# A two-layer RWKV-7/mLSTM trunk on one core: the planner may go straight on to a small product that is due within one K tile, the program begins and ends differently, and two lags change

## The chip, the cores and the metric

The kernel runs on one core of one Trainium2 chip. The metric is the device time of a whole execution in microseconds (us). Three runs of the kernel before gave 2409.18, 2411.95 and 3999.0 us, median 2411.95.

## The reference

A trunk of two layers works on 512 frames of 1024 features, all in fp32. Each layer is a half-weighted SwiGLU block, a mixer block in which two token mixers (RWKV-7 with 8 heads of 64, mLSTM with 4 heads of 128) read one joint projection, and a second half-weighted SwiGLU block; a last RMSNorm follows.

```
for l in range(DEPTH):
    h = h + HALF * _swiglu(_rmsnorm(h, ffn1_norm[l]), ffn1_w_in[l], ffn1_w_out[l])
    xn = _rmsnorm(h, mix_norm[l])
    z = xn @ w_in[l]
    ...
    u = jax.nn.sigmoid(g_a) * (y_a @ br_a[l]) + jax.nn.sigmoid(g_b) * (y_b @ br_b[l])
    h = h + u @ w_out[l]
    h = h + HALF * _swiglu(_rmsnorm(h, ffn2_norm[l]), ffn2_w_in[l], ffn2_w_out[l])
return _rmsnorm(h, final_norm)
```

## The kernel before, in words

Activations lie transposed: features on the 128 partitions, the 512 frames along the free axis. A projection makes one block of 128 output features. Its weight block comes by DMA as `wraw`; ScalarE (ACT) rounds it to `whi`, VectorE (DVE) takes the rest `wlo` (`cut`, L425 and L426). For each of the 8 blocks of 128 input features (a K tile) TensorE (PE) then does three products, hi·hi, hi·lo and lo·hi (`product`, L461 to L463), into one PSUM bank. Two banks (pool `mm`) take projections, six (pool `mx`) everything small.

The program has five kinds of stages: `opening` (L437), where the first two weight blocks and the input arrive in pieces; the rest of the first SwiGLU (`ffn`); `mixers`; a second `ffn`; and after two layers the end in `run` (L1262 and on), a norm and eight multiplications, each followed by its DMA out.

In `mixers` a planner (`Weave`) writes TensorE's order out by hand. The small products (transposes, products of 64, 32 or 16 rows, sums over partitions) are threads that yield what they wait for: a time on the planner's own clock `t` ("at"), a flag, a lock or a projection. The planner resumes the first thread that is ready and, where none is, writes one K tile of a projection and adds `STEP` = 0.69 us to `t`. It charges 0.1 us for each turn from K tiles to small products and 0.1 us back. The "at" times come from lags written into the code: `wv.mark(latency, busy)` books DVE's time and returns the start plus the latency; ACT's queue is not booked. The other engines' orders follow from the order in which the code issues their instructions and from the scheduler.

The threads that the prediction speaks of: `mlstm_gates` (its lag of 16.0 stands ahead of the transposes of `rstd` and `ee`, helper line L684); `rwkv_chunks` (lag 3.2 between transposes and `rwkv_values`, L1163); `rwkv_gated` (L1231 and on: sums over heads by `sums`, L482 and L483, a subtraction L1238, a square L1239, a second `sums`, then `rsqrt`, which is Ln L517 and Exp L518, each behind a load of ACT's function table); `mlstm_head` (scores L798, their Relu and Exp L795 and L796); and `rwkv_out` (L1194, L1206 and the chain of states L1212, with copies L1199 that give its `mx` banks back). `table` (L511) asks for an Ln on a constant, to have the Ln table loaded early.

Of the kernel before, what the change touches and what calls it, by code (L numbers as in the profile page):

```python
# [13 lines left out]
AF = mybir.ActivationFunctionType  # L14
ALU = mybir.AluOpType
# [3 lines left out]
P = 128  # L19
# [4 lines left out]
KD = D // P  # L24
# [206 lines left out]
class Weave:  # L231
# [49 lines left out]
    def run(self):  # L281
        trunk = self.trunk
        job = None
        self.threads.sort(key=lambda th: th[0])
        while job or any(not th[3] for th in self.threads):
            th = next((th for th in self.threads if self.ready(th[2])), None)
            if th is not None:
                if th[2][0] == "lock":
                    self.held.add(th[2][1])
                self.resume(th)  # L290
                continue
            if job is None:
                th = next((th for th in self.threads if th[2][0] == "proj"), None)
                if th is not None:
                    job = [th, trunk.weights(th[2][1]), trunk.mm(), 0]
                    th[2] = ("job", None)
                    self.mark(0.0, 1.4)
            if job is not None:
                th, w, ps, k = job
                trunk.product(ps, w, k, trunk.xh[:, k, :], trunk.xl[:, k, :], k == 0, k == KD - 1)  # L300
                self.t += self.STEP + (0.1 if self.small else 0.0)
                self.small = False
                job[3] += 1
                if job[3] == KD:
                    job = None
                    self.resume(th, ps)
                continue
            times = [th[2][1] for th in self.threads if th[2][0] == "at"]
            times += [self.flags[th[2][1]] for th in self.threads if th[2][0] == "flag" and th[2][1] in self.flags]
            self.t = min(times)  # L310
# [19 lines left out]
class Trunk:  # L330
    def __init__(self, ctx, tc, a, out):
        self.tc, self.nc, self.a, self.out = tc, tc.nc, a, out
        pool = lambda n, b, **k: ctx.enter_context(tc.tile_pool(name=n, bufs=b, **k))
        self.pw = pool("weights", 3)
        self.pt = pool("tmp", 2)
        self.pmm = pool("mm", 2, space=PSUM)
        self.pmx = pool("mx", 6, space=PSUM)
        self.pd = pool("dram", 1, space=DRAM)
        self.keep = Scope(tc)
        nc = self.nc  # L340
        k = self.keep.tile
        self.xh = k((P, KD, T), F32R, "xh")
        self.xl = k((P, KD, T), F32R, "xl")
        self.rstd = k((P, T), F32, "rstd")
        self.acc = k((P, T), F32, "acc")
        self.cst = k((P, 4, P), F32, "cst")
        self.sel = k((P, 7, P), F32R, "sel")
        self.big = k((P, 512), F32, "big")
        self.fin = k((P, KD), F32, "fin")
        self.tid = k((P, 8, 16), F32, "tid")  # L350
        self.vec = [k((P, NCOL), F32, f"vec{l}") for l in range(L)]
        self.half = [k((P, NCOL), F32, f"half{l}") for l in range(L)]
        self.k256 = [k((P, 4), F32, f"k256_{l}") for l in range(L)]
        self.eps = k((P, 4), F32, "eps")
        self.onemu = [k((P, 15), F32, f"onemu{l}") for l in range(L)]

        k((P, 96), F32, "pad")
        self.sq, self.sl = (k((P, 512), F32R, n) for n in ("sq", "sl"))
        self.ld = [k((P, 512), F32, f"ld{i}") for i in range(2)]
        self.residual()  # L360
        for i, e in enumerate((RMS_EPS, GN_EPS, LN_EPS)):
            nc.gpsimd.memset(self.eps[:, i : i + 1], e)
        nc.scalar.copy(out=self.eps[:, 3:4], in_=self.eps[:, 0:1])
        nc.sync.dma_start(out=self.vec[0], in_=a["vec"][0])
        self.ident = self.cst[:, 0, :]
        dram = lambda n, k, s: [self.pd.tile(s, F32, name=f"{n}{i}", tag=f"{n}{i}") for i in range(k)]
        self.vfirst = dram("vfirst", 4, [P, T])
        self.bonus = dram("bonus", 4, [P, T])
        self.yd = dram("yd", 8, [P, T])
        self.hd = dram("hd", KD, [P, T])  # L370
        self.mxd = dram("mxd", 4, [64, 16, 16])
        self.gd = dram("gd", 16, [P, T])
        self.zd = dram("zd", 4, [P, 8, 16])
# [63 lines left out]
    def opening(self):  # L437

        nc, a = self.nc, self.a
        raw = [self.pw.tile([P, KD * P], F32, name="wraw", tag="wraw", bufs=2) for _ in range(2)]  # L440
        w = [self.parts() for _ in range(2)]
        ps = [self.mm() for _ in range(2)]
        for k in range(0, KD, 2):
            for i in (k, k + 1):
                (nc.gpsimd if i % 2 else nc.sync).dma_start(out=self.h[:, i, :], in_=a["xt"][:, i, :])
                self.feed(i, self.col(0, "g1", i))
                if i == k:
                    for j in range(2):
                        s = slice(k * P, (k + 2) * P)
                        nc.sync.dma_start(out=raw[j][:, s], in_=a["f1i"][0, 0, j, :, s])  # L450
                        self.cut(raw[j], w[j], k, k + 2)
            for i in (k, k + 1):
                for j in range(2):
                    self.product(ps[j], w[j], i, self.xh[:, i, :], self.xl[:, i, :], i == 0, i == KD - 1)
        return ps

    def product(self, ps, w, k, xh, xl, first, last):
# [52 lines left out]

    def table(self):  # L511

        self.nc.scalar.activation(out=self.eps[:, 3:4], in_=self.eps[:, 0:1], func=AF.Ln)

    def rsqrt(self, out, in_, eps, scale=1.0):
        nc = self.nc
# [11 lines left out]
    def ffn(self, l, m, done, first=None):  # L528
        nc = self.nc
        win, wout = self.a[f"f{m}i"], self.a[f"f{m}o"]  # L530
        sc = Scope(self.tc)
        hh = [sc.tile((P, T), F32R, f"hh{j}") for j in range(KF)]
        hl = [sc.tile((P, T), F32R, f"hl{j}") for j in range(KF)]
        for j in range(KF):
            if j == 0 and first is not None:
                pg, pu = first()
                self.norm()
            else:

                pg = self.project(win[l, j, 0], ps=self.mx() if j < 2 else None)  # L540
                if j == 0:
                    self.norm()
                pu = self.project(win[l, j, 1])
            if j == 2 and first is not None:
                self.constants()
            g = self.tmp("t0")
            nc.vector.tensor_tensor(out=g, in0=pg, in1=self.rstd, op=ALU.mult)  # L547
            s = self.tmp("t1", 1)
            nc.scalar.activation(out=s, in_=g, func=AF.Silu)  # L549
            p = self.tmp("t2", 1)  # L550
            nc.vector.tensor_tensor(out=p, in0=pu, in1=s, op=ALU.mult)  # L551
            self.split(hh[j], hl[j], p)
        for i in range(KD):
            ps = self.mm()
            for k0 in range(0, KF, KD):
                nk = min(KD, KF - k0)
                w = self.weights(wout[l, i, :, k0 * P : (k0 + nk) * P], nk)
                for k in range(nk):
                    j = k0 + k
                    self.product(ps, w, k, hh[j], hl[j], j == 0, j == KF - 1)  # L560
            t = self.tmp("t0")
            nc.vector.scalar_tensor_tensor(out=t, in0=ps, scalar=0.5, in1=self.rstd, op0=ALU.mult, op1=ALU.mult)
            nc.vector.tensor_tensor(out=self.h[:, i, :], in0=self.h[:, i, :], in1=t, op=ALU.add)  # L563
            done(i)
        sc.close()
# [136 lines left out]
    def mlstm_gates(self):  # L702

        nc, l, zm, wv = self.nc, self.l, self.zm, self.wv
# [18 lines left out]
        self.split(self.m_rc[I], self.m_rc[F], rc[I])  # L723
        nc.vector.tensor_tensor(out=rt[I], in0=rt[I], in1=rc[I], op=ALU.subtract)
        nc.scalar.activation(out=slab[F], in_=rt[I], func=AF.Exp)
        yield "at", wv.mark(16.0, 8.0)

        ps = self.mx()
        self.transposes(ps, [self.rstd[:, P * j : P * j + P] for j in range(4)])
        nc.vector.tensor_copy(out=self.m_rcol, in_=ps.rearrange("p (j c) -> p j c", j=4)[:, :, 0:1])  # L730
        ps = self.mx()
# [291 lines left out]
    def rwkv_chunks(self, p):  # L1023

        nc, l, k, a, kk, bk, wv = self.nc, self.l, self.r_k, self.r_a, self.r_kk, self.r_bk, self.wv
# [28 lines left out]
        at = wv.t + 3.0  # L1054
        for q in range(2):
# [14 lines left out]
            for hh in range(2):  # L1070
# [1 line left out]
                C = slice(8 * hh + 4 * q, 8 * hh + 4 * q + 4)  # L1072
                nc.scalar.copy(out=s3[0:64, C, wc : wc + CH], in_=ps4[0:64, :, wc : wc + CH])
                nc.scalar.copy(out=s3[64:128, C, yc : yc + CH], in_=ps4[64:128, :, yc : yc + CH])
            at = wv.t + 3.2
        yield "at", at
        self.rwkv_values(p)

# [183 lines left out]
    def run(self):  # L1262
# [39 lines left out]
        self.norm(self.last)  # L1302
        for i in range(KD):
            h = self.h[:, i, :]
            eng = nc.gpsimd if i in (2, 5) else nc.vector
            eng.tensor_tensor(out=h, in0=h, in1=self.rstd, op=ALU.mult)
            nc.sync.dma_start(out=self.out[i * P : i * P + P, :], in_=h)
        self.hs.close()
        self.keep.close()

# [10 lines left out]
```

## Time and profile before

| | us |
|---|---|
| median of three runs | 2411.95 |
| the profiled execution | 2413.39 |
| its span, first to last instruction | 2411.7 |
| PE busy | 2379.0 (99% of the span) |
| DVE busy | 1301.7 (54%) |
| ACT busy | 1062.1 (44%) |
| POOL busy | 109.4 (5%) |
| first product starts at | 8.21 |
| first of the last two matmuls starts at | 2397.57 |

The span is 1.7 us shorter than the profiled execution's time; the rest lies outside the first and last instruction. Matmuls are pipelined and their ends are modelled, so the distance between two starts tells what a matmul takes, and its duration does not. The first layer's mixers lie roughly between 380 and 750 us and the second's between 1570 and 1960 us.

### The profile page before, as it was taken

How to read it: one execution, taken by the hardware profiler on the slowest of the kernel's cores; microseconds unless marked ns; L12 is line 12 of the kernel's file. 1: busy time of each engine (PE TensorE's matmuls, PEld its weight loads, DVE VectorE, ACT ScalarE, POOL GpSimd, SP SyncE). 2: the span in 40 equal slices, each digit the busy share in tenths (PEclk: the TensorE clock that was granted, in tenths of full speed). 3: DMA queues.
4: the chain of work that ended last, by engine and by line, in shares of the span. 5: the costliest groups of instructions: out<-in, count | busy, mean ns of one | idle time of the engine just before them, and what ended most of it. 6: DMA issues, size and time to landing. Idle time of an engine off the chain costs nothing.

```text
span 2411.7 us, 33612 instructions
## 1 busy us (share of the span) xinstructions
PE 2379.0 (99%) x13044; PEld 1954.2 (81%) x13044; DVE 1301.7 (54%) x2340; ACT 1062.1 (44%) x1808; POOL 109.4 (5%) x155
## 2 busy tenths in 40 slices
PE   8999999999999999999999999999999999999997
PEld 7888888787788888888888888878877888888886
DVE  5444446876866644444444444478678665444433
ACT  5333336566565443333343333375565645333322
POOL 1000000000000100000000000000000001000012
PEclk9999999999999999999999999999999999999999
DMA  4223333323436322233323333433133353332332
GB/s 159 96 97 96 106 117 117 99 80 91 129 94 185 118 96 96 96 95 97 102 94 99 99 95 111 132 94 106 60 117 119 100 156 128 99 100 98 92 97 83
DMA packets 116799, 256.13 MB, mean 106 GB/s; under 512 B 40064, under 2 KB 43264, under 8 KB 116640
## 3 DMA queue, kind: packets, MB, share of 16 engines
q1 hardware_dynamic: 115696, 251.30, 33.5%
q8 instruction: 103, 1.69, 0.3%
q10 hardware_dynamic: 624, 1.64, 0.2%
q0 software_dynamic: 320, 1.05, 0.1%
q14 instruction: 56, 0.46, 0.1%
HBM read 230.88 MB, written 23.07 MB: 105 GB/s over the span
## 4 chain that ended last, share of the span: by engine, by line
PE 88%; DVE 6%; ACT 3%; issue 2%; DMA 1%; POOL 0%; DVEq 0%; SPq 0%; ACTq 0%; POOLq 0%
PE mm L461 27%; PE mm L463 26%; PE mm L462 26%; PE mx L1194 1%; DVE wlo L426 1%; PE mx L813 1%; PE mx L684 1%; PE mx L798 1%; PE mx L463 1%; PE mx L462 1%; PE mx L461 1%; DVE tz L1102 0%; DVE pr L1100 0%; PE mx L1182 0%; DVE qk L758 0%
## 5 line engine op out<-in xcount | busy, mean ns | idle before, releaser
L425 ACT CAST whi<-wraw 128x512 fp32r<-128x512 f32 (+1 forms) x800 | 487.2, 610 | 1030.1 <-PE mm L462 920.3
L426 DVE TENSOR_TENSOR wlo<-wraw,whi 128x512 fp32r<-128x512 f32 (+1 forms) x800 | 556.7, 697 | 593.3 <-ACT whi L425 590.2
L461 PE MATMUL mm<-xh,whi 128*128 128x512 f32 x2104 | 837.5, 398 | 8.2 <-ACT whi L425 8.2
L463 PE MATMUL mm<-xh,wlo 128*128 128x512 f32 x2104 | 822.7, 391 | 2.1 <-DVE wlo L426 2.1
L462 PE MATMUL mm<-xl,whi 128*128 128x512 f32 x2104 | 821.8, 391 | 0.0
L461 PEld LDWEIGHTS mm<-xh,whi 128*128 128x128 f32 x2104 | 396.6, 189 | 96.1 <-ACT whi L425 8.2
L463 PEld LDWEIGHTS mm<-xh,wlo 128*128 128x128 f32 x2104 | 396.3, 188 | 87.3 <-DVE wlo L426 2.9
L462 PEld LDWEIGHTS mm<-xl,whi 128*128 128x128 f32 x2104 | 396.8, 189 | 79.9 <-issue 1.2
L463 PE MATMUL mm<-hh,wlo 128*128 128x512 f32 x704 | 273.9, 389 | 0.0
L461 PE MATMUL mm<-hh,whi 128*128 128x512 f32 x704 | 273.9, 389 | 0.0
L462 PE MATMUL mm<-hl,whi 128*128 128x512 f32 x704 | 273.9, 389 | 0.0
L462 PEld LDWEIGHTS mm<-hl,whi 128*128 128x128 f32 x704 | 132.1, 188 | 27.6
L461 PEld LDWEIGHTS mm<-hh,whi 128*128 128x128 f32 x704 | 132.1, 188 | 27.5
L463 PEld LDWEIGHTS mm<-hh,wlo 128*128 128x128 f32 x704 | 132.1, 188 | 27.2
L551 DVE TENSOR_TENSOR t<-mm,t 128x512 f32<-128x512 f32 x88 | 60.8, 691 | 135.3 <-PE mm L463 130.6
L547 DVE TENSOR_TENSOR t<-mm,rstd 128x512 f32<-128x512 f32 x81 | 56.0, 691 | 125.0 <-PE mm L463 122.6
L509 POOL TENSOR_TENSOR acc<-acc,t 128x512 f32<-128x512 f32 x36 | 47.9, 1329 | 1197.2 <-ACT t L507 1183.9
L549 ACT ACTIVATE t<-t 128x512 f32<-128x512 f32 x88 | 55.7, 633 | 27.8 <-DVE t L547 27.6
L488 ACT CAST hh<-t 128x512 fp32r<-128x512 f32 x88 | 54.7, 622 | 23.6 <-DVE t L551 23.6
L489 DVE TENSOR_TENSOR hl<-t,hh 128x512 fp32r<-128x512 f32 x88 | 60.9, 692 | 7.6
L496 ACT ACTIVATE xh<-h,vec 128x512 fp32r<-128x512 f32 x48 | 34.4, 724 | 44.0 <-DVE h L563 35.2
L497 DVE SCALAR_TENSOR_TENSOR xl<-h,vec,xh 128x512 fp32r<-128x512 f32 x48 | 35.7, 751 | 29.6 <-ACT xh L496 29.5
(267 smaller groups left out, 2177.2 us busy)
## 6 DMA issues: line engine op xcount, KB each, us to landing
wraw<-wi SPq DMA_DIRECT2D x94, 512.0 KB, 3.5
wraw<-f2i SPq DMA_DIRECT2D x88, 512.0 KB, 3.3
wraw<-f1i SPq DMA_DIRECT2D x86, 512.0 KB, 3.3
wraw<-f1o SPq DMA_DIRECT2D x32, 512.0 KB, 3.6
wraw<-f2o SPq DMA_DIRECT2D x32, 512.0 KB, 3.5
gd<-t SPq DMA_DIRECT2D x32, 256.0 KB, 3.1
wraw<-br SPq DMA_DIRECT2D x32, 256.0 KB, 3.0
wraw<-wo SPq DMA_DIRECT2D x16, 512.0 KB, 3.3
```

What stands on the lines that cost most here:

```text
L425: nc.scalar.copy(out=hi, in_=raw)
L426: nc.vector.tensor_tensor(out=lo, in0=raw, in1=hi.bitcast(F32), op=ALU.subtract)
L461: nc.tensor.matmul(ps, lhsT=hi, rhs=xh, start=first, stop=False)
L462: nc.tensor.matmul(ps, lhsT=hi, rhs=xl, start=False, stop=False)
L463: nc.tensor.matmul(ps, lhsT=lo, rhs=xh, start=False, stop=last)
L488: nc.scalar.copy(out=hi, in_=x)
L489: nc.vector.tensor_tensor(out=lo, in0=x, in1=hi.bitcast(F32), op=ALU.subtract)
L497: nc.vector.scalar_tensor_tensor(out=self.xl[:, i, :], in0=h, scalar=gain, in1=self.xh[:, i, :].bitcast(F32), op0=ALU.mult, op1=ALU.subtract)
L509: eng.tensor_tensor(out=self.acc, in0=self.acc, in1=sq, op=ALU.add)
L547: nc.vector.tensor_tensor(out=g, in0=pg, in1=self.rstd, op=ALU.mult)
L549: nc.scalar.activation(out=s, in_=g, func=AF.Silu)
L551: nc.vector.tensor_tensor(out=p, in0=pu, in1=s, op=ALU.mult)
```

## The change

In the planner: after a small product, if a thread is due within one `STEP`, the clock `t` is set to that time and the thread goes on, where before a K tile would have been written first. Two lags change: 16.0 to 18.5 in `mlstm_gates`, 3.2 to 4.0 in `rwkv_chunks`. The Ln that `table` asks for now reads `acc`, which other work writes, and so cannot be moved far ahead of its place.

At the beginning the small vector comes by ACT's queue, two products on a cleared tile `ld` are written ahead of the first real one, the input and the weight blocks all come by SP's queue in the order in which they are used, and a third projection of the first SwiGLU is written ahead of its norm. At the end all eight multiplications are DVE's and the DMAs out alternate between SP's and ACT's queues.

```diff
+            if self.small:
+                due = [th[2][1] for th in self.threads if th[2][0] == "at"]
+                due += [self.flags[th[2][1]] for th in self.threads if th[2][0] == "flag" and th[2][1] in self.flags]
+                if due and min(due) <= self.t + self.STEP:
+                    self.t = min(due)
+                    continue
             if job is not None:
                 th, w, ps, k = job
...
-        nc.sync.dma_start(out=self.vec[0], in_=a["vec"][0])
+        nc.scalar.dma_start(out=self.vec[0], in_=a["vec"][0])
+
+        nc.gpsimd.memset(self.ld[0], 0.0)
+        for _ in range(2):
+            nc.tensor.matmul(self.mx(), lhsT=self.ld[0][:, 0:P], rhs=self.ld[0], start=True, stop=True)
...
+        for k0, k1 in ((0, 2), (2, 4), (4, KD)):
+            block(0, k0, k1)
+            at(k0)
+            block(1, k0, k1)
+            for i in range(k0 + 1, k1):
+                at(i)
+        for k0, k1 in ((0, 2), (2, 4), (4, 6), (6, KD)):
+            self.feed(k0, self.col(0, "g1", k0))
+            for j in range(2):
+                self.cut(raw[j], w[j], k0, k1)
+            products(k0)
+            for i in range(k0 + 1, k1):
                 self.feed(i, self.col(0, "g1", i))
...
-        self.nc.scalar.activation(out=self.eps[:, 3:4], in_=self.eps[:, 0:1], func=AF.Ln)
+        self.nc.scalar.activation(out=self.eps[:, 3:4], in_=self.acc[:, 0:1], func=AF.Ln)
...
             if j == 0 and first is not None:
                 pg, pu = first()
+                second = self.project(win[l, 1, 0], ps=late())
                 self.norm()
...
-        yield "at", wv.mark(16.0, 8.0)
+        yield "at", wv.mark(18.5, 8.0)
...
-            at = wv.t + 3.2
+            at = wv.t + 4.0
...
-            eng = nc.gpsimd if i in (2, 5) else nc.vector
-            eng.tensor_tensor(out=h, in0=h, in1=self.rstd, op=ALU.mult)
-            nc.sync.dma_start(out=self.out[i * P : i * P + P, :], in_=h)
+            nc.vector.tensor_tensor(out=h, in0=h, in1=self.rstd, op=ALU.mult)
+            (nc.scalar if i % 2 else nc.sync).dma_start(out=self.out[i * P : i * P + P, :], in_=h)
```

The lines of the changed kernel lie 24 or 28 lower down: L461 to L463 are L485 to L487 there, L482 and L483 are L506 and L507, L684 is L712, L798 is L826, L1194 is L1222, L1206 is L1234, L1199 is L1227.

PE in the first layer's mixers, where the fourth pair of RWKV heads meets an mLSTM head. Before, from the first sums of `rwkv_gated` to the start of the K tiles after its second sums:

```order
L482 MATMUL mx<-sq,sel 128x512
L483 MATMUL mx<-sl,sel 128x512
L1182 MATMUL mx<-s_3210,mn_3202 64x128 x16
L461 MATMUL mm<-xh,whi 128x512
L462 MATMUL mm<-xl,whi 128x512
L463 MATMUL mm<-xh,wlo 128x512
L798 MATMUL mx<-qk 128x256
L798 MATMUL mx<-qk 128x128
L1194 MATMUL mx<-rbx_3206,s_3210 128x128 x8
L482 MATMUL mx<-sq,sel 128x512
L483 MATMUL mx<-sl,sel 128x512
L461 MATMUL mm<-xh,whi 128x512
```

The same place in the changed kernel, from the first sums to the head's last scores:

```order
L506 MATMUL mx<-sq,sel 128x512
L507 MATMUL mx<-sl,sel 128x512
L1222 MATMUL mx<-rbx_3209,s_3213 128x128 x8
L819 MATMUL mx<-rc,sel 128x512
L826 MATMUL mx<-qk 128x512
L826 MATMUL mx<-qk 128x384
L506 MATMUL mx<-sq,sel 128x512
L507 MATMUL mx<-sl,sel 128x512
L1222 MATMUL mx<-rbx_3209,s_3213 128x128 x8
L1234 MATMUL mx<-s_3213,rbx_3209 64x64 x14
L826 MATMUL mx<-qk 128x256
L826 MATMUL mx<-qk 128x128
```

The K tile between the two sums and the two behind the second sums have left this stretch; nothing but small products stands in it. The second layer has the changed piece twice.

ACT at that place, from the rounding of the square that the second sums read. Before:

```order
L488 CAST sq<-acc 128x512
L1185 ACTIVATE s_3210<-mx 64x512
L796 ACTIVATE ee_3267<-ee_3267 128x256
L795 ACTIVATE ee_3271<-mx,gem 128x128
L796 ACTIVATE ee_3271<-ee_3271 128x128
L517 ACT_TABLE_LOAD
L517 ACTIVATE acc<-mx,eps 128x512
L1199 COPY avr_3198<-mx 64x4x64 x2
L518 ACT_TABLE_LOAD
L518 ACTIVATE acc<-acc 128x512
L1199 COPY avr_3198<-mx 64x4x64
```

And in the changed kernel:

```order
L512 CAST sq<-acc 128x512
L823 ACTIVATE ee_3270<-mx,gem 128x512
L1227 COPY avr_3201<-mx 64x4x64
L824 ACTIVATE ee_3270<-ee_3270 128x512
L823 ACTIVATE ee_3274<-mx,gem 128x384
L541 ACT_TABLE_LOAD
L541 ACTIVATE acc<-mx,eps 128x512
L824 ACT_TABLE_LOAD
L824 ACTIVATE ee_3274<-ee_3274 128x384
L542 ACTIVATE acc<-acc 128x512
L1227 COPY avr_3201<-mx 64x4x64 x2
```

The two copies that empty `mx` banks stood between the two table loads; they now stand behind both and behind two Exps.

PE around the transposes that wait for the changed lag of `mlstm_gates`, in the first layer. Before:

```order
L684 MATMUL mx<-cst,bk 128x128 x4
L684 MATMUL mx<-cst,rstd 128x128 x4
L684 MATMUL mx<-cst,ee_3267 128x128 x4
L684 MATMUL mx<-cst,avr_3176 128x128 x4
L461 MATMUL mm<-xh,whi 128x512
```

And in the changed kernel:

```order
L712 MATMUL mx<-cst,bk 128x128 x4
L485 MATMUL mm<-xh,whi 128x512
L486 MATMUL mm<-xl,whi 128x512
L487 MATMUL mm<-xh,wlo 128x512
L485 MATMUL mm<-xh,whi 128x512
L486 MATMUL mm<-xl,whi 128x512
L487 MATMUL mm<-xh,wlo 128x512
L712 MATMUL mx<-cst,avr_3179 128x128 x4
L712 MATMUL mx<-cst,rstd 128x128 x4
L712 MATMUL mx<-cst,ee_3270 128x128 x4
```

Two K tiles and the four transposes of `avr` now stand ahead of `rstd` and `ee`, and one more K tile stands ahead of `bk`. Over the program the stretches of small products between K tiles go from 167 to 149 (the two new products at the start make one of the 149); the count of K-tile products, 9360, stays.

## Rows read from the trace of the kernel before

**Rows 1.** The page, busy time by engine: busy us (share) xinstructions.

```profile
PE 2379.0 (99%) x13044; PEld 1954.2 (81%) x13044; DVE 1301.7 (54%) x2340; ACT 1062.1 (44%) x1808; POOL 109.4 (5%) x155
```

**Rows 2.** PE's waits: who <- released by: us in total, times, longest.

```profile
PE mm L461 <- ACT whi L425: 8.2, 1, 8.2
PE mx L684 <- ACT ee L725: 3.8, 2, 2.9
PE mm L463 <- DVE wlo L426: 2.1, 2, 1.9
PE mx L1163 <- ACT s L1074: 1.6, 3, 0.7
```

**Rows 3.** Timeline, opening: start us, us, engine, line, operation, tiles [idle before].

```profile
6.53 1.33 ACT L496 ACTIVATE xh<-h,vec 128x512 fp32r<-128x512 f32 x2 [2.27 <-DMA h<-xt]
...
13.19 0.63 PE L463 MATMUL mm<-xh,wlo 128*128 128x512 f32 x1
...
13.61 0.63 PE L461 MATMUL mm<-xh,whi 128*128 128x512 f32 x1
...
22.15 1.02 PE L523 MATMUL mx<-acc,cst 128*128 128x512 f32 x2
```

**Rows 4.** Timeline of the end: multiplications and DMAs out.

```profile
2401.56 5.86 DVE L1306 TENSOR_TENSOR h<-h,rstd 128x512 f32<-128x512 f32 x6 [4.76 <-ACT rstd L518]
2402.82 5.29 SPq L1307 DMA_DIRECT2D out_dram<-h  x8
```

**Rows 5.** L1306's instructions on DVE: shortest/median/longest in ns, first and last start.

```profile
L1306 DVE TENSOR_TENSOR h<-h,rstd x6: 677/679/1789, 2401.6 to 2406.7; 128x512 f32<-128x512 f32 x6
```

**Rows 6.** PE's timeline around one stretch of small products in the mixers.

```profile
476.60 0.39 PE L463 MATMUL mm<-xh,wlo 128*128 128x512 f32 x1
476.92 1.19 PE L1146 MATMUL mx<-mn,t1p 32*32 32x32 f32 x32
478.05 0.50 PE L461 MATMUL mm<-xh,whi 128*128 128x512 f32 x1
478.38 0.40 PE L462 MATMUL mm<-xl,whi 128*128 128x512 f32 x1
```

**Rows 7.** PE's timeline where the fourth RWKV pair meets an mLSTM head.

```profile
705.95 0.39 PE L463 MATMUL mm<-xh,wlo 128*128 128x512 f32 x1
706.18 0.40 PE L791 MATMUL mx<-rc,sel 128*128 128x512 f32 x1
...
707.62 0.69 PE L482 MATMUL mx<-sq,sel 128*128 128x512 f32 x1
...
711.45 0.81 PE L798 MATMUL mx<-qk 128*128 128x256 f32 x4
712.10 1.95 PE L1194 MATMUL mx<-rbx,s 128*128 128x128 f32 x16
...
715.74 1.95 PE L1194 MATMUL mx<-rbx,s 128*128 128x128 f32 x16
717.62 1.03 PE L1206 MATMUL mx<-s,rbx 128*64 128x64 f32 x28
```

**Rows 8.** ACT's timeline at the same place.

```profile
711.35 0.59 ACT L1185 ACTIVATE s<-mx 64x512 f32<-64x512 f32 x1
...
714.12 1.28 ACT L517 ACT_TABLE_LOAD   x1
...
716.13 0.76 ACT L1199 COPY avr<-mx 64x256 f32<-64x256 f32 x2
...
718.19 0.63 ACT L518 ACTIVATE acc<-acc 128x512 f32<-128x512 f32 x1
```

**Rows 9.** Windows, mixers: us, busy (x) PE PEld DVE ACT POOL, clock, DMA, GB/s.

```profile
427.20:430.70 3.50, 1.48 (x11) 1.41 (x12) 2.80 (x5) 3.42 (x6) 0.13 (x1) 1.00 0.15 40
...
1625.40:1628.80 3.40, 3.40 (x10) 2.62 (x9) 2.79 (x12) 2.85 (x6) 0.00 (x0) 0.50 0.51 164
...
1843.80:1847.30 3.50, 3.47 (x8) 2.82 (x9) 3.50 (x7) 0.00 (x0) 0.00 (x0) 0.51 0.42 129
```

More of the change, by code (lines that the diff above doesn't have):

```diff
@@ L442, in opening, with block, products @@
         ps = [self.mm() for _ in range(2)]
-        for k in range(0, KD, 2):
-            for i in (k, k + 1):
-                (nc.gpsimd if i % 2 else nc.sync).dma_start(out=self.h[:, i, :], in_=a["xt"][:, i, :])
-                self.feed(i, self.col(0, "g1", i))
[L447 to L454, printed above, removed]
+        at = lambda i: nc.sync.dma_start(out=self.h[:, i, :], in_=a["xt"][:, i, :])
+        def block(j, k0, k1):
+            s = slice(k0 * P, k1 * P)
+            nc.sync.dma_start(out=raw[j][:, s], in_=a["f1i"][0, 0, j, :, s])
+        def products(i):
+            for j in range(2):
+                self.product(ps[j], w[j], i, self.xh[:, i, :], self.xl[:, i, :], i == 0, i == KD - 1)
+        for k0, k1 in ((0, 2), (2, 4), (4, KD)):
[6 more added lines that the diff above has]
+            self.feed(k0, self.col(0, "g1", k0))
+            for j in range(2):
+                self.cut(raw[j], w[j], k0, k1)
+            products(k0)
+            for i in range(k0 + 1, k1):
+                self.feed(i, self.col(0, "g1", i))
+                products(i)
         return ps
@@ L534, in ffn @@
         for j in range(KF):
+            late = lambda: self.mx() if j < 2 else None
             if j == 0 and first is not None:
                 pg, pu = first()
+                second = self.project(win[l, 1, 0], ps=late())
                 self.norm()
+            elif j == 1 and first is not None:
+                pg, pu = second, self.project(win[l, j, 1], ps=late())
             else:
-                pg = self.project(win[l, j, 0], ps=self.mx() if j < 2 else None)
+                pg = self.project(win[l, j, 0], ps=late())
                 if j == 0:
```

## The prediction

> **What bounds the kernel now.** The page's first line comes first: PE is busy in 99% of the span, DVE in 54% and ACT in 44% [rows 1]. The time is thus PE's list of products plus the few stretches in which PE stands still, and an edit counts only as far as it changes one of these. PE's waits come second [rows 2]: 8.2 us before the first product, 3.8 where four transposes wait for `ee` (L684), 2.1 for a weight block, 1.6 for RWKV's L1163. All waits in the mixers together are a handful of microseconds, so the old planner nearly always had something ready, and there is little standing time that a better order could win. Third come the timelines of the opening, the end and one meeting of two threads, where ACT's list tells how long the answer to a small product takes. Last, the granted clock by windows.
>
> The profiled execution took 2413.39 us, 1.4 more than the median of the runs shown, 2411.95. The differences below are made against the profiled execution and applied to the median. All are small: 2% of this kernel are 48 us, about what a measurement of it can tell from no change.
>
> **The change part by part.**
>
> *Opening.* PE's first product stands 8.2 us in [rows 2], behind two L496 from 6.53 on; ACT had idled 2.27 us for `xt` [rows 3]. In the new order the first pieces are alone at the head of SP's queue, and the second L496, some 0.67 of the 1.33, no longer stands ahead of the first rounding: 2.27 + 0.67 = 2.9 off the start. From 8.2 to the norm's product at 22.15 are 13.9 us for 48 products, which at 0.23 (705.95 to 706.18, [rows 7]) would take 11.0; 2.9 are lost, since the first products stand 0.42 apart (13.19 to 13.61), at the lower clock. The two dummy products may have raised the clock by then, but eight pieces of input and weights must then come faster than before: I give back 1.4 of the 2.9. The third projection put ahead of the norm covers the norm's chain and keeps PE's count of products. Sum **−4.3**; bounds −2.3 (only the DMA wait goes) to −5.8 (all of both).
>
> *End.* DVE's six multiplications take 5.86 us [rows 4] with a median of 0.68 and a longest of 1.79 [rows 5], held up while POOL does its two. Eight at 0.68 are 5.4: −0.4. Issues on SP last until 2402.82 + 5.29 = 2408.11, 0.7 after the last multiplication; two queues share them: −0.6. Sum **−1.0** (0 to −1.8).
>
> *Fewer turns.* From the last K-tile product to a small one is 0.32 (476.60 to 476.92), from the first K-tile product back to the second 0.33 [rows 6], where 0.23 is the pace: a turn costs 0.1 in and 0.1 back. Of 167 stretches 149 are left: 18 × 0.2 = **−3.6** (half of it to all).
>
> *The two lags.* In front of the waits for `ee` now stand three K tiles more, partly one ahead of `bk`, and a group of transposes: at 3 × 3 × 0.23 = 2.1 plus some 0.6 they cover the 2.9 us of the longer wait but for 0.2, and the shorter (3.8 − 2.9 = 0.9) wholly: −3.5. Lag 4.0 puts off L1163 by up to one K tile; half of its 1.6: −0.8. Sum **−4.3** (−3 to −5.4). The displaced K tiles cost nothing; they are only done earlier.
>
> *Three clusters.* Where `rwkv_gated` meets an mLSTM head, K tiles have left PE's list, once in the first layer and twice in the second. What is left must wait for ACT and DVE. Before, from the first sums (707.62) to the end of the last Exp (718.19 + 0.63) were 11.2 us, in which ACT did, among others, L1185 at 0.59, two table loads of 1.28 and two L1199 copies in 0.76 [rows 8]. In the new order the L1185 leave and wider Relus and Exps of the head and one more copy come in, about the same sum, and the two copies that free `mx` banks stand behind both loads. PE's own work inside is the two sums twice (0.5 each), L1194 twice at 1.9 (715.74 to 717.62), L791 with the wide L798 (706.18 to 707.62: 1.4), L1206 at 1.0 and the last L798 at up to 0.65 [rows 7]: about 7.6. So PE stands 11.2 − 7.6 = 3.6 us where it had K tiles to do: 3 × 3.6 = **+10.8**. Bounds per cluster: 0, if the chain's first part is over before PE arrives, since the old lists waited hardly at all there; 4.3, if the copies too (0.76) come wholly on top.
>
> The Trainium skill, "ScalarE: Activation LUTs", section "Table sets: the hidden batching unit", says that ln followed by exp needs one load, because one set has both functions, and that is less than this chain pays. The trace differs: L517 and L518 have a load each, of 1.28 us [rows 8]. By the rule a cluster would cost 3.6 − 1.28 = 2.3, the three together +7.0 in place of +10.8, and the time would be 2418.
>
> *The jumps elsewhere.* The rule sets the planner's clock forward 42 times, by 12.65 us in all, counted with the planner's own numbers; some 14 of these, 3 us, lie in the clusters. Each jump is a wait on PE if the lags are exact, in place of a K tile that would have covered it. Lags too long by a little cost nothing; ACT, which the planner does not book, makes others too short. Bounds 0 and 28 × 0.69 = 19; I take **+9.0**, near the planner's 9.6, since the 1.6 and 3.8 us of waits [rows 2] show that most lags were long enough and a few were not.
>
> *Clock.* Two stretches of 3.4 to 3.5 us in the mixers ran at a granted 0.50, that is at 1.2 GHz [rows 9]; half of each is lost, 1.7. The one at 1625 follows waits on L1163, the one at 1843 the 1.9 us wait for `wlo` [rows 2]. But the 2.9 us wait near 427 left the clock at 1.00, though PE did 1.48 us of work in 3.50. So waits can, but need not, cost twice. Two more such stretches: **+3.2** (0 to 8).
>
> Sum: −4.3 − 1.0 − 3.6 − 4.3 + 10.8 + 9.0 + 3.2 = +9.8. On the median that is **2421.8**; on the profiled execution it would be 2423.2.
>
> **The rivals.**
>
> *The merge pays.* If the small products that were due within one K tile are in truth ready (lags on the safe side, as the small waits in [rows 2] suggest), clusters and jumps cost nothing and the rest stays: −13.2, 2398.8. For it: of 167 stretches only a few show a wait. Against it: in the old order K tiles stood there and covered, so the lack of waits then is no sign that the answers were early; and the order really shows PE with nothing else to do. It needs ACT's chain of 11.2 to shrink to 7.6. Chance 0.20, at 2394 to 2404.
>
> *Both halves cancel.* Jumps cost half, 4.5, clusters 2 each, clock 1.5: −13.2 + 12 = about −1, 2411. At 2404 to 2412, chance 0.14.
>
> *The clock falls after most new waits.* Some ten of the new waits, each followed by 1.7 us of loss as at 1843: +17 in place of +3.2, 2435.6, with full jumps more, up to 2442. For it: two of the old waits were followed by 0.50. Against it: the longest was not. It decides from about six such stretches on. Chance 0.06, above 2434.
>
> The Trainium skill, "TensorE: Matmul & The Clock Gate", section "A second HAM failure mode: psum-queue depth-cycling", describes this: short idles between groups of matmuls make the clock go to and fro and cost throughput. The trace agrees in two of the three windows of [rows 9] and disagrees in one.
>
> That the change does not do what it says is excluded for the order: 18 stretches have gone. It may hold for the opening, if the clock is not raised, which the bound −2.3 takes in.
>
> **How the numbers follow.** My forecast, waits that outweigh what is gained, has the chance 0.60 and runs from 2412 to 2434: the upper end is opening −2.3, end 0, turns −1.8, lags −3, clusters 3 × 4.3, jumps 12.6, clock 4, together +22.4. The rest is the three rivals'. The range **2401 to 2434** takes in the case in which both cancel and the upper part of the first rival; left out are most of that one, 0.14, and the clock's, 0.06. Faster by 48 us would take more than three times all the gains together: 0.01. Slower by 48 would need the clock to fall after nearly every jump: 0.03. Within 2%: 0.96. On the sign alone: slower than before 0.66.
>
> **What would show it.** The first product should start at 5.3 to 6 us and the norm's product of the first layer come after 72 products at about 23.5. Waits of PE on `mx` in the mixers should rise by some 15 to 20 us over those of before, the largest new ones behind L1199's copies, Ln and Exp at three places, on L1222 and L826 by their new lines. The waits for `ee` should be under 1 us. Stretches at a granted 0.50 in the mixers should number four in place of two. The forecast is wrong if the waits on `mx` rise by less than 5 us, which makes it the first rival, or if the sum of waits is as said and the time is still lower, which would mean that the turns cost more than 0.2.

## The result and the profile after

The changed kernel took a median of 2425.25 us over six runs (2421.39 to 2427.9), the kernel before, beside it, 2412.21: a ratio of 1.0055, 95% interval 1.0045 to 1.0065. It is 13.0 us slower; 9.8 were forecast. One of the six runs before was a slow one of 3999.0 us; the median of the other five is 2411.95, and the ratio goes by these. The profiled execution of the changed kernel took 2421.39 us, the shortest of its six, against 2413.39 before: +8.0. So 8 us can be read from the two traces, and the other 5 lie between these two executions and the medians (3.9 for the changed kernel, 1.2 for the one before). Over the six runs the mean granted clock goes with the time: 0.997 at 2421.39, 2421.89 and 2424.04, 0.996 at 2426.46, 0.995 at 2427.64 and 2427.9.

Where the 8 us lie is told first by cutting both programs at the norms, which begin every stage. Windows of the kernel before, first and second layer's mixers with their projections (us, busy by engine with counts, clock, DMA share, GB/s):

```profile
376.65:847.86 471.21, 465.90 (x3348) 378.88 (x3346) 333.38 (x701) 272.37 (x484) 25.64 (x46) 1.00 0.37 113
1567.75:2040.67 472.92, 468.16 (x3351) 381.97 (x3350) 342.73 (x715) 274.48 (x491) 23.25 (x43) 0.99 0.35 111
```

And of the changed kernel:

```profile
373.18:849.41 476.23, 467.08 (x3347) 379.86 (x3346) 336.73 (x701) 270.14 (x483) 27.75 (x46) 1.00 0.36 109
1569.31:2050.49 481.18, 468.13 (x3352) 378.69 (x3350) 343.75 (x715) 272.43 (x490) 24.12 (x43) 1.00 0.35 108
```

The mixers begin 3.5 us earlier (376.65 to 373.18: the opening), lose 5.0 in the first layer and 8.3 in the second, and the end gives 1.8. The SwiGLU blocks between them have not moved by 0.1. PE's busy time in them rose by 1.2 us only, the sum of the windows by 13.3: PE stands. What it stands for is in its waits (who <- released by: us, times, longest), where [rows 2] had 3.8 on `ee` at the head:

```profile
PE mx L826 <- ACT avr L1227: 8.4, 5, 2.0
PE mm L487 <- DVE wlo L437: 2.4, 2, 1.8
PE mx L712 <- ACT t L795: 1.5, 2, 1.3
...
PE mx L826 <- ACT v L801: 1.2, 1, 1.2
PE mm L485 <- DVE zt L605: 1.1, 1, 1.1
PE mx L1191 <- ACT s L1102: 1.0, 3, 0.4
...
PE mx L712 <- ACT ee L753: 0.4, 1, 0.4
```

The waits that the lags were to remove have shrunk (3.8 to 0.4 and 1.6 to 1.0). In their place the head's scores (L826) wait 8.4 us for copies by ACT. One of the three large ones, in PE's timeline of the first layer, which answers to [rows 7]:

```profile
703.36 0.50 PE L507 MATMUL mx<-sl,sel 128*128 128x512 f32 x1 [0.22 <-DVE sl L513]
703.70 1.95 PE L1222 MATMUL mx<-rbx,s 128*128 128x128 f32 x16
705.57 1.04 PE L1234 MATMUL mx<-s,rbx 128*64 128x64 f32 x28
706.60 0.70 PE L826 MATMUL mx<-qk 128*128 128x256 f32 x2
709.34 0.49 PE L826 MATMUL mx<-qk 128*128 128x128 f32 x2 [2.05 <-ACT avr L1227]
709.67 0.33 PE L1240 MATMUL mx<-st,gt 128*128 128x64 f32 x2
```

ACT at the same time, against [rows 8]:

```profile
704.56 1.28 ACT L541 ACT_TABLE_LOAD   x1
705.85 0.69 ACT L541 ACTIVATE acc<-mx,eps 128x512 f32<-128x512 f32 x1
706.56 1.28 ACT L824 ACT_TABLE_LOAD   x1
707.85 0.52 ACT L824 ACTIVATE ee<-ee 128x384 f32<-128x384 f32 x1
708.28 0.61 ACT L542 ACTIVATE acc<-acc 128x512 f32<-128x512 f32 x1
708.92 0.76 ACT L1227 COPY avr<-mx 64x256 f32<-64x256 f32 x2
```

ACT is never idle there: the copies that would free PE's bank stand behind 4.4 us (704.56 to 708.92) of Ln, two loads and two Exps. The same picture, with the same 2.05, stands at 1746 and 1916 in the second layer. These are the three clusters of the forecast.

The opening and the end, against [rows 3] and [rows 4]:

```profile
5.03 0.49 PE L485 MATMUL mm<-xh,whi 128*128 128x512 f32 x1 [0.18 <-ACT xh L520]
...
24.11 1.02 PE L547 MATMUL mx<-acc,cst 128*128 128x512 f32 x2
...
2411.28 4.91 DVE L1333 TENSOR_TENSOR h<-h,rstd 128x512 f32<-128x512 f32 x8 [4.67 <-ACT rstd L542]
2412.00 3.94 SPq L1334 DMA_DIRECT2D out_dram<-h  x4
2412.60 3.95 ACTq L1334 DMA_DIRECT2D out_dram<-h  x4
```

The first product starts at 5.03 in place of 8.2, the norm's product at 24.11 after 72 products (before at 22.15 after 48). Eight multiplications take 4.91 us where six took 5.86.

### The profile page after: what moved, and what is told of

The parts are those of the page before. It is cut to its first block, busy times and chain, and to the rows that moved or that the text cites. A ratio compares the mean times of both kernels' runs of the same rounds, so it can differ in the third digit from the quotient of the medians.

```text
span 2419.7 us, 33606 instructions
## 1 busy us (share of the span) xinstructions
PE 2382.3 (98%) x13048; PEld 1950.7 (81%) x13048; DVE 1304.9 (54%) x2342; ACT 1059.7 (44%) x1808; POOL 107.5 (4%) x150
## 4 chain that ended last, share of the span: by engine, by line
PE 84%; DVE 8%; ACT 5%; issue 1%; DMA 1%; SPq 0%; DVEq 0%; ACTq 0%
PE mm L485 26%; PE mm L486 26%; PE mm L487 26%; DVE wlo L437 1%; PE mx L841 1%; PE mx L486 1%; PE mx L487 1%; PE mx L485 1%; DVE pr L1128 1%; DVE tz L1130 1%; PE mx L1222 0%; ACT L541 0%; DVE qk L786 0%; ACT whi L436 0%; PE mx L712 0%
## 5 line engine op out<-in xcount | busy, mean ns | idle before, releaser
L485 PE MATMUL mm<-xh,whi 128*128 128x512 f32 x2096 | 830.3, 396 | 2.4 <-DVE zt L605 1.1
L487 PE MATMUL mm<-xh,wlo 128*128 128x512 f32 x2096 | 817.7, 390 | 2.5 <-DVE wlo L437 2.4
L485 PEld LDWEIGHTS mm<-xh,whi 128*128 128x128 f32 x2096 | 393.7, 188 | 91.3 <-issue 7.7
L487 PEld LDWEIGHTS mm<-xh,wlo 128*128 128x128 f32 x2096 | 393.6, 188 | 87.2 <-DVE wlo L437 4.2
L485 PE MATMUL mm<-hh,whi 128*128 128x512 f32 x704 | 273.9, 389 | 0.0
L487 PE MATMUL mm<-hh,wlo 128*128 128x512 f32 x704 | 273.9, 389 | 0.0
L487 PEld LDWEIGHTS mm<-hh,wlo 128*128 128x128 f32 x704 | 132.1, 188 | 27.5
L485 PEld LDWEIGHTS mm<-hh,whi 128*128 128x128 f32 x704 | 132.1, 188 | 27.4
L485 PE MATMUL mm<-yh,whi 128*128 128x512 f32 x128 | 49.8, 389 | 0.0
```

What stands on the lines that cost most here:

```text
L485: nc.tensor.matmul(ps, lhsT=hi, rhs=xh, start=first, stop=False)
L487: nc.tensor.matmul(ps, lhsT=lo, rhs=xh, start=False, stop=last)
```

## The experiments

The kernel before ran beside each group of four: medians 2413.14, 2413.23 and 2412.9. "Changed" stands for the changed kernel, 2425.25, measured beside the 2412.21; as these medians of one kernel differ by up to 1 us, a difference between kernels of two groups is known to about 1 us.

**1. The rule taken out** (opening, end and new lags stay).

```diff
-                if due and min(due) <= self.t + self.STEP:
-                    self.t = min(due)
-                    continue
```

> The changed kernel with the planner's rule taken out; the new opening, end and lags stay. Theory (the rule's waits on PE cost more than the turns give back; the rest of the change pays): opening -3.5 and end -1.8 as the traces before and after show, lags about -4 from the waits for ee and s: 2403 against 2412 before, and PE's waits over 0.15 us in the mixers back to about 6 us from 21.5. Rival A (the loss is in the lags or the new opening, the rule is neutral): 2420 or more. Rival C (the loss is mostly the lower clock after waits): the time also falls, but in the profile the waits have shrunk by less than half of what the time has, and the rest is stretches at 0.50.

2406.78 us, ratio 0.9976 (0.9965 to 0.9986): 18.5 below the changed kernel. Rival A is out. So is rival C: PE's waits in the mixers (those over 0.15 us) are 9.6 us in place of the changed kernel's 21.5, and these 11.9 are most of the 14.7 by which the profiled execution is shorter. The mixers' windows are 473.5 and 469.3 us. The size of the rest was overstated: 6.4 us below before, not 9, and the waits did not fall to 6, as some came back elsewhere. PE's wait on the chain of states, in the profile of this kernel, where before it was 0.9:

```profile
PE mx L1234 <- DVE st L1237: 4.8, 7, 2.1
```

**2. The rule alone** on the kernel before.

```diff
+            if self.small:
+                due = [th[2][1] for th in self.threads if th[2][0] == "at"]
...
+                if due and min(due) <= self.t + self.STEP:
+                    self.t = min(due)
+                    continue
```

> The kernel before with the rule alone; old opening, old end, old lags. Theory: the whole loss and none of the gains: the mixers' +13 that the trace shows, with the lags' gain of about 4 gone, so 2412 + 17 to 22 = 2429 to 2434. Rival A (rule neutral): 2412 within 3.

2418.01, ratio 1.0019 (1.0011 to 1.0028): 4.9 slower: not 17 to 22, and not neutral either, as rival A had it. The parts do not add: the rule gives +4.9, the rest -6.4, both together +13.0. By this trace the rule even gains in the first layer's mixers (468.0 against 471.2) and loses in the second's (479.5 against 472.9), where two of the three clusters stand.

**3. The rule only for what is due within 0.15 us.**

```diff
-                if due and min(due) <= self.t + self.STEP:
+                if due and min(due) <= self.t + 0.15:
```

> The changed kernel, but the rule acts only where the next thread is due within 0.15 us and not 0.69: by the planner's own numbers 9 jumps of 0.5 us in all in place of 42 of 12.65 us. Theory (a jump costs what it skips, and the K tile that it displaces would have covered it): within 1.5 us of the kernel without the rule, about 2403. Rival B (a merge costs by itself, whatever its length, since one engine's answer is always late): 9/42 of the loss, some 4 to 5 us above the kernel without the rule.

2408.37, ratio 0.9978 (0.9970 to 0.9987): 1.6 above the kernel without the rule. That is next to the theory's 1.5 and far from rival B's 4 to 5: the short jumps are nearly free.

**4. The copies that free the banks moved to DVE.**

```diff
-                nc.scalar.copy(out=y[O, Q], in_=ps4[O, :, 0:CH])
+                nc.vector.tensor_copy(out=y[O, Q], in_=ps4[O, :, 0:CH])
```

> The changed kernel with the copies at L1227, which free the mx banks, on DVE in place of ACT, so that they no longer stand behind two table loads and two Exps. Theory (at the three clusters PE waits 2.05 us each for these copies, and 1.65 and 0.6 at two more): the 8.4 us of waits of L826 on these copies go, about 6 us of it is kept: 2419 against 2425. Rival D (ACT's chain of loads binds PE at the next step anyway): the wait moves to another row and the time falls by under 2 us.

2426.23, ratio 1.0056 (1.0044 to 1.0069): nothing gained; the theory fails, and the time stays, as rival D said. The wait of 2.05 on them became one of 2.40 on the next group of products, L1240. DVE and PE at the first cluster of this kernel:

```profile
709.62 0.69 DVE L1275 TENSOR_TENSOR avr<-avr,acc 128x512 f32<-128x512 f32 x1 [1.39 <-ACT acc L542]
...
710.23 0.28 DVE L1243 TENSOR_SCALAR st<-mx,dc 128x64 f32<-128x64 f32 x1
...
710.57 0.43 PE L1240 MATMUL mx<-st,gt 128*128 128x64 f32 x2 [2.40 <-DVE st L1243]
```

L1243, for which PE waits, needs nothing of the normalisation; it stands behind L1275 in DVE's queue, and L1275 waits for the last Exp (L542) on ACT. So with the copies on DVE the chain through the two loads still reaches PE, by another queue. But this second way was opened by the edit: in the changed kernel's own DVE queue the same L1243 is done ahead of L1275.

```profile
706.66 0.28 DVE L1243 TENSOR_SCALAR st<-mx,dc 128x64 f32<-128x64 f32 x1 [0.27 <-PE mx L1234]
...
708.95 0.68 DVE L1275 TENSOR_TENSOR avr<-avr,acc 128x512 f32<-128x512 f32 x1
```

The changed kernel's PE waits by way of the copies alone, and what their place in ACT's queue is worth, with DVE's order kept, stays open.

**5. Both lags back at 16.0 and 3.2** (rule, opening and end stay).

```diff
-        yield "at", wv.mark(18.5, 8.0)
+        yield "at", wv.mark(16.0, 8.0)
...
-            at = wv.t + 4.0
+            at = wv.t + 3.2
```

> The changed kernel with the two lags back at 16.0 and 3.2; rule, opening and end stay. The rule alone cost 5 us, the rest of the change alone gave 6, and both together cost 13: something is not additive. Theory (the new lags shift the planner's clock so that the rule merges at worse places, in the first layer above all): the mixers as with the rule alone, 947.5 us by its trace against 957.4, so 2418.0 - 3.5 - 1.8 = 2412.7. Rival A (the lags' gain on the waits for ee holds under the rule too): 2425 + 3.5 = 2428.

2412.22, ratio 0.9999 (0.9990 to 1.0007), against 2412.7 expected; rival A's 2428 is out. The lags, worth a gain by their waits, cost 13.0 us together with the rule. Their place is the first layer; windows of this kernel:

```profile
373.06:840.97 467.91, 463.50 (x3348) 379.39 (x3346) 332.63 (x701) 267.48 (x481) 25.29 (x46) 1.00 0.38 113
1560.86:2040.61 479.75, 468.77 (x3352) 380.10 (x3351) 343.51 (x715) 272.60 (x490) 24.22 (x43) 1.00 0.35 109
```

467.91 in place of 476.23, with the first layer's cluster gone and the second's two still there. The cluster is a part of these 8.3 us; PE's waits in that layer fell by 4.6 in all (8.85 to 4.22), and a stretch at the lower clock is worth 1.7.

**6. The loads taken out.** The Ln of `rwkv_gated` becomes an Identity: this kernel leaves the logarithm out of the eight normalisations, and with it their table loads.

```diff
-        self.rsqrt(gn, ps, self.eps[:, 1:2])
+        nc.scalar.activation(out=gn, in_=ps, func=AF.Identity, bias=self.eps[:, 1:2])
+        nc.scalar.activation(out=gn, in_=gn, func=AF.Exp, scale=-0.5)
```

> The changed kernel, but rwkv_gated's Ln is an Identity with a bias and its Exp stays: the eight normalisations of the RWKV heads miss their logarithm (this part of the computation is changed), and the table loads around it go; order and number of products stay. Theory (at the three clusters the two loads of 1.28 us stand ahead of what PE waits for, by way of ACT's copies or of DVE's queue): 2.57 us less there, the three waits of 2.05 go with what hides behind modelled ends, about -7: 2418. Rival D (the chain of sums, square and sums binds without the loads too): under -2, 2423 or more.

2413.31, ratio 1.0002 (0.9993 to 1.0012): 11.9 below the changed kernel with the same number of products. PE at the second cluster of this kernel:

```profile
1738.84 0.50 PE L507 MATMUL mx<-sl,sel 128*128 128x512 f32 x1 [0.22 <-DVE sl L513]
1739.17 1.95 PE L1222 MATMUL mx<-rbx,s 128*128 128x128 f32 x16
1741.05 1.04 PE L1234 MATMUL mx<-s,rbx 128*64 128x64 f32 x28
1742.02 0.92 PE L826 MATMUL mx<-qk 128*128 128x256 f32 x4
1743.37 0.43 PE L1240 MATMUL mx<-st,gt 128*128 128x64 f32 x2 [0.43 <-DVE st L1243]
```

From L507 to L1240 are 4.53 us (1738.84 to 1743.37); in the changed kernel's first cluster, above, L826's last products begin only at 709.34, 5.98 behind L507, and L1240 follows at 709.67: 6.31. The other clusters of both kernels show the same 4.53 and 6.31. So a cluster loses 1.8 us to the loads, 5.3 for three. The spans differ by 6.1 (2419.7 to 2413.6). The other 6 of the 11.9 are between executions: all runs of this kernel had a clock of 0.997 or 0.998, half of the changed kernel's 0.995 or 0.996. That the clock falls less often because there are fewer long waits fits this, but is not shown: in the two profiled executions it is the kernel without loads that ran more of the mixers at 0.50 (6.8 us against 3.4).

**7. The rule in the first layer alone, with the old lags.**

```diff
-            if self.small:
+            if self.small and trunk.l == 0:
...
```

> Old lags, new opening and end, and the rule in the first layer alone. By the trace of the rule alone the first layer's mixers take 468.0 us in place of 471.2, the second's 479.5 in place of 472.9. Theory (what a merge gives depends on what stands at its place): 2413 - 3.5 - 1.8 - 3.2 = 2404.7, ahead of every version so far. Rival B (every merge costs, and 468.0 was the chance of one execution): 2407 or more.

2404.90, ratio 0.9964 (0.9952 to 0.9977), against 2404.7: it beats both kernels, and rival B is out. The same rule gains in the first layer and loses in the second: in both it was number 5's 2412.22, in neither number 11's 2407.87.

**8. Without the two dummy products.**

```diff
-        nc.gpsimd.memset(self.ld[0], 0.0)
-        for _ in range(2):
-            nc.tensor.matmul(self.mx(), lhsT=self.ld[0][:, 0:P], rhs=self.ld[0], start=True, stop=True)
```

> The changed kernel without the two products on a cleared tile at the beginning. Theory (they raise the clock ahead of the first real product): the clock rises some 6 to 8 us later and the norm's product of the first layer, at 24.1 us in the changed kernel, comes 1.5 to 3 us later; the rest is unchanged. Rival E (the pieces of the input set the pace there, not the clock): under 0.5 us later.

One execution, 2424.38 us, inside the changed kernel's own 2421.39 to 2427.9. PE at the norm's product:

```profile
24.29 1.02 PE L544 MATMUL mx<-acc,cst 128*128 128x512 f32 x2
```

That is 0.2 later than with them. Rival E holds. The products at the lower clock (0.43 apart up to 9.6 us) fill time in which the pieces of the input would have been waited for anyway: by 15 us 32 products have started, against 33 in the changed kernel. The other traces say the same. In those of numbers 9, 11 and 12, which have the two products, the clock rose only at 9.5 to 10.6 us, and the norm's product came at 24.05 to 24.55; in the eight others that have them it rose by 5.9 us, and the product came at 23.93 to 24.49.

**9 and 10. One lag at a time.** In 9 only 18.5 is new, in 10 only 4.0; against the changed kernel:

```diff
-            at = wv.t + 4.0
+            at = wv.t + 3.2
```

```diff
-        yield "at", wv.mark(18.5, 8.0)
+        yield "at", wv.mark(16.0, 8.0)
```

> The changed kernel with only the lag of mlstm_gates at 18.5; that of rwkv_chunks back at 3.2. Its product order differs from that with both old lags by 38 rows, from the changed kernel by 344. Theory (the lag 4.0 moves the rule's merges to worse places in the first layer, the lag 18.5 does what it is for): 2412.2 with both old lags, less the waits for ee of 3.8 - 0.4, is 2409. Rival F (it is the lag 18.5 that spoils the order): 2420 or more.

> The changed kernel with only the lag of rwkv_chunks at 4.0; that of mlstm_gates back at 16.0. Its product order differs from the changed kernel by 20 rows, from that with both old lags by 362. Theory: the changed kernel's time with the waits for ee back, 2425 + 3.4 = 2428. Rival F: 2415 or less.

Only 4.0: 2428.47, ratio 1.0065 (1.0053 to 1.0078), as expected; this lag alone costs 16 us under the rule. Only 18.5: 2416.35, ratio 1.0013 (1.0004 to 1.0022), 7 above the expectation and 4 above both old lags: a miss, though rival F's 2420 is not reached. In the first layer it gained (467.1 us); the second took 484.9, 5.1 more than with both old lags. There a wait came back ahead of RWKV's values. PE at that place, and the window behind it, of this kernel:

```profile
1617.01 0.33 PE L1191 MATMUL mx<-s,mn 64*64 64x64 f32 x2 [2.21 <-ACT s L1102]
```

```profile
1617.50:1624.30 6.80, 6.52 (x27) 5.24 (x28) 5.10 (x21) 3.13 (x6) 0.00 (x0) 0.50 0.33 118
```

2.21 us of waiting, then 6.8 us at a granted 0.50, of which half is lost. With a second stretch, of 3.4 us at 1740 behind a cluster, the lower clock costs 5.1 us in this layer, against 1.7 in number 5's. So 3.4 of the 5.1 are the clock's, and may be this execution's alone.

**11. Opening and end alone**: the edits of numbers 1 and 5 together.

```diff
-                if due and min(due) <= self.t + self.STEP:
...
-        yield "at", wv.mark(18.5, 8.0)
+        yield "at", wv.mark(16.0, 8.0)
```

> New opening and end alone: no rule, old lags. Theory (opening -3.5, end -1.8): 2413.2 - 5.3 = 2407.9; the two lags without the rule are then worth 1 us against the 2406.8 of the kernel without the rule. Rival G (the lags are worth their waits, 4 us, also without the rule): 2411.

2407.87, ratio 0.9980 (0.9971 to 0.9989), as expected; rival G's 2411 is out. So opening and end give 5.0, and the two lags without the rule 1.1 more (2406.78), hardly clear of the 1 us above. All with the new opening and end: without the rule 2407.87 (old lags) and 2406.78 (new), with it 2412.22 and 2425.25. The rule costs 4.4 us with the old lags and 18.5 with the new.

**12. The better order of each layer.** Rule with old lags in the first, new lags without the rule in the second.

```diff
-            if self.small:
+            if self.small and trunk.l == 0:
...
-        yield "at", wv.mark(18.5, 8.0)
+        yield "at", wv.mark(18.5 if self.l else 16.0, 8.0)
...
-            at = wv.t + 4.0
+            at = wv.t + (4.0 if self.l else 3.2)
```

> New opening and end; in the first layer the rule with the old lags, in the second the new lags without the rule, the better mixers of each by the traces (468.6 and 469.3 us). Theory (a layer's mixers keep the time of their own order): 2404.9 less the second layer's 472.5 - 469.3 = 3.2, of which 1.7 was a stretch at the lower clock: 2402 to 2403.5. Rival H (the layers are not independent, since the second's start depends on the first's end): 2405 or more.

2403.73, ratio 0.9965 (0.9953 to 0.9978): 9 us below before, just above the theory's 2402 to 2403.5 and below rival H's 2405. Its mixers took 470.29 and 469.42 us. It has the lowest median, but against number 7 the intervals overlap, so which of the two is faster stays open.

## Why the prediction was right

The likeliest case came: PE's new waits outweigh what the rest gives. Sign and size held (13.0 for 9.8), though one step, the two lags, failed outright and others were off by half or more. By its own terms, on the two profiled executions (+8.0):

- *Opening* -4.3: measured -3.5. The start was right (5.03 for 5.3). Of the 2.9 that the lower clock had seemed to cost, 1.5 were counted as gained (with the 2.9 of the start that makes 4.4, not 4.3); 0.3 was, and number 8 shows why: the pieces of the input would have been waited for.
- *End* -1.0: measured -1.8. A multiplication still lasts 0.69, but they overlap and start 0.60 apart, so eight take 4.91 and not 5.4. The first two of the six before took 1.79 and 1.74, for as long as POOL did its two.
- *Fewer turns* -3.6: at most 1.5. Added up from start to start in both traces, waits and the lower clock left out, the K-tile products of the mixers took 1.5 us less. A turn is cheaper than [rows 6] made it: over the mixers before, the first product behind a group takes 0.32 and the last ahead of one 0.26 on average, where 0.23 is the pace, so 0.12 and not 0.2. At its own end a group gains nothing by the merge. This one takes as long ahead of another group as ahead of a K tile, in the changed kernel:

```profile
471.55 1.19 PE L1174 MATMUL mx<-mn,t1p 32*32 32x32 f32 x32
472.67 0.66 PE L712 MATMUL mx<-cst,bk 128*128 128x128 f32 x4
...
527.91 1.19 PE L1174 MATMUL mx<-mn,t1p 32*32 32x32 f32 x32
529.04 0.50 PE L485 MATMUL mm<-xh,whi 128*128 128x512 f32 x1
```

 1.12 and 1.13 us from start to start. Against the 1.5 stands a rise that no term had: the small products of the mixers took 4.9 us more, start to start.
- *The two lags* -4.3: this step failed. The waits went as said (5.4 to 1.4). Their time did not come back: without the rule the lags are worth 1.1, since PE then waits for the chain of states instead (4.8 us in number 1, 0.6 in number 11), and under the rule they cost 13.0 (the lag 4.0 alone 16, 18.5 alone 4), as 4.0 sends the planner along another order in the first layer. The step took the waits of the old order as if the rest of the order stood still.
- *Three clusters* +10.8: about 8.8, by the mechanism that was named. They stand where the order said, with 2.05 us of wait for the copies each, 6.2 together; the two loads are 1.8 of each. PE at the second cluster of the changed kernel, and ACT's rounding of `sq` in it:

```profile
1735.21 0.48 PE L506 MATMUL mx<-sq,sel 128*128 128x512 f32 x1
...
1737.47 0.48 PE L819 MATMUL mx<-rc,sel 128*128 128x512 f32 x1
...
1739.58 0.51 PE L506 MATMUL mx<-sq,sel 128*128 128x512 f32 x1
1740.30 0.51 PE L507 MATMUL mx<-sl,sel 128*128 128x512 f32 x1 [0.22 <-DVE sl L513]
...
1746.29 0.49 PE L826 MATMUL mx<-qk 128*128 128x128 f32 x2 [2.05 <-ACT avr L1227]
1738.91 0.62 ACT L512 CAST sq<-acc 128x512 fp32r<-128x512 f32 x1
```

 From the first sums to the head's last scores pass 11.1 us (11.2 forecast, without the copies). The waits that show are 2.27. L819 and the wide L826 take 2.11 to the second sums, against 1.44 in [rows 7]: these sums wait until `sq` is ready at 1739.53, and as a matmul's end is modelled, the 0.67 shows as no wait. So PE stands about 2.9 of the forecast 3.6, and its own work, some 8.1, was the term set too low, at 7.6 (its parts as listed add up to 7.85). By the Trainium skill's page "ScalarE: Activation LUTs", section "Table sets: the hidden batching unit", one load would have been enough for Ln and Exp; the trace shows two of 1.28 us each time, and what their absence is worth was measured.
- *Jumps elsewhere* +9.0: PE's waits in the mixers rose by 11.5 us in all (10.0 to 21.5 by adding up the waits). Less the clusters' 6.2 and the lags' -4.0 that leaves 9.3. That short jumps cost next to nothing was shown by number 3; that each longer one costs what it skips was not measured one by one. The 4.9 us by which the small products stand further apart do not show as waits: 2.0 are the 0.67 of the three clusters, and where the rest lies stays open.
- *Clock* +3.2: in the profiled pair -1.7, one stretch in place of two [rows 9]; over the runs about +3, if all of the 5 us between the profiled pair and the medians is the clock's. One stretch follows a cluster, the other two clusters pass without; windows of the changed kernel:

```profile
710.90:714.30 3.40, 3.40 (x11) 2.41 (x9) 1.64 (x4) 2.16 (x6) 2.23 (x3) 0.50 0.25 60
1746.30:1749.70 3.40, 3.40 (x18) 2.77 (x18) 1.90 (x6) 2.67 (x7) 2.09 (x3) 1.00 0.00 0
```

 The same wait of 2.05 us can be followed by 1.2 GHz or by 2.4. In the fourteen profiles of this case, 14 of 35 waits of at least 1.8 us inside the mixers were followed by such a stretch, and 9 of the 23 stretches there followed no wait of that length.

That the sum came so near the result is in part luck: on the profiled pair the clusters cost 4.6 less than forecast in waits that show and the clock 4.9 less, while the turns gained 2.1 less and the small products cost 4.9 that were in no term. The signs named ahead came in part: the wait for `ee` (0.4) and the first product (5.03) as said or better, the norm's product a little late (24.11 for 23.5), but PE's waits on `mx` rose by 9.9 and not by 15 to 20 (7.6 to 17.6), and one stretch at 0.50 stood in the mixers, not four.

The first rival, that the merge pays, is refuted for the program and true for a layer: with the old lags the rule gains about 3 us in the first. What decides is not the rule but which answers are late at the places to which it leads.

## What to carry to other kernels

An order that a planner writes is not a sum of its edits: price the list that comes out, not the rule and the constants that went in, and try the edits one by one, since a constant that removes a wait here can cost several times as much under another rule. Going straight on to work that is due soon was nearly free here where it was due at once (number 3), and dear where the answer came through ACT, whose queue the planner does not book (number 6). When a wait is named after one copy, look at what stands ahead of it in its queue before moving it: moved to another engine, it can put the next answer there behind the same chain (number 4).

## What was not expected of the hardware

The lower clock came after some waits and not after others: at one and the same place with one and the same wait of 2.05 us the granted clock was 0.50 in one layer and 1.00 in the other, and the six runs of one program spread over 6.5 us with means from 0.995 to 0.997. And more than a third of such stretches (9 of 23) followed no wait of 1.8 us or more. A merge of two groups of small products saved less than it seemed: the last product of a group takes 0.19 us on average to a group of another kind, against 0.14 to a K tile (mixers before, all kinds together, waits left out).
